# Binding the modulation's VectorE operations behind named operations, and spreading them over the block pairs

## The chip, the cores and the metric

The kernel runs on one core of a Trainium2 chip. Its time is device microseconds of one execution; several executions are shown by their median. A profiled execution leaves a trace of every instruction of the engines: TensorE (PE: matmuls; PEld: its weight loads), VectorE (DVE), ScalarE (ACT), GpSimd (POOL) and SyncE (SP, which here only issues transfers).

## The reference: what is computed

A transformer of two layers (width 1024, FFN width 2816) works on 256 latent tokens and 256 context tokens. Layer 0 mixes the tokens with a short convolution, layer 1 with grouped-query attention; an FFN stands before and after each mixer. Every sublayer is modulated by vectors that come from the conditioning:

```python
mod = (jax.nn.silu(c) @ mod_w[i] + mod_b[i]).reshape(bsz, 3, 3, 1, D_MODEL)
modc = (jax.nn.silu(c_ctx) @ mod_w[i] + mod_b[i]).reshape(3, 3, D_MODEL)
lat = lat + 0.5 * mod[:, 0, 2] * _swiglu(
    _modulate(lat, norm_g[i, 0], mod[:, 0, 0], mod[:, 0, 1]), ffn_w13[i, 0], ffn_w2[i, 0])
```

`_modulate` is an RMS norm scaled by (1 + scale) and shifted; `_swiglu(h, w13, w2)` is (silu(gate) * up) @ w2. The products are in float32. `mod` and `modc` together need nine chunks of 1024 numbers for each layer, one set for the latent and one for the context stream.

## The kernel before

**Products.** Each float32 operand is split into a high and a low part. `split` (L107) writes the high part with ScalarE (L108) and the low part with VectorE (L109), and a product is three matmuls: high by high (L137), high by low (L138), low by high (L139), in `mm3`. Weights come in as raw float32 tiles `wr` of 128x1024 (`load_raw`, L102, issued on SP at L104) from a ring of eight buffers, and are split into `wh` and `wl`.

**The FFN** (`ffn`, L768) takes the hidden blocks in three thirds of 8, 7 and 7. For each block the first product gives gate and up, VectorE multiplies them to `gm`, and `gm` is split into `gh` and `gl`. After each third, the second product (`project`, L575, accumulating in `py`) adds that third's share to all 8 output tiles m; `finish` (L553) then updates the residual `x` on VectorE (L559), gated by the modulation.

In the three FFNs with 512 tokens most blocks are computed as a "block pair" (`Pair`, L686 on): a fast-multiplication scheme with seven products of 12 matmuls of 128x256 in place of eight. Its steps `head`, `five`, `six`, `seven` and `four` are interleaved with those of the pair before. The sums of weights run on VectorE (L717, L725), a negation on POOL (L695) with a transfer issued on POOL (L698), sums of products on VectorE (L754, L759), the product `gm` (L765), then the split into `gh` and `gl`.

**The modulation.** The vectors of chunk 2 of layer 0 and later are computed by VectorE while TensorE does the FFNs. One unit, `mod_unit` (L173), is one VectorE operation of 128x1024 (L179, written out as `junk`): it multiplies a transposed weight tile with the broadcast conditioning and sums along the row into one column of `mod`. There are 224 units; two raw tiles (`load_mod`, from the same ring `wr`, issued on SP) feed four units, or two units where only the latent stream is needed.

**What sets the order.** Units wait in a list. `tick(n)` (L216) adds n to an account and issues a unit for every whole one; it is called after each block pair, after each finished tile of the second product, and in the other stages. `gate_of` and `scale_of` issue units themselves if a vector that is needed is not done. The program is written in the order of the code, but a planner then lays out each engine's instructions, by its own estimate of when operands come and engines are free; so an independent unit can land far from the place of its tick. `tc.issue_after(op)` ties instructions on the same engine to come after `op` in that engine's order, without a semaphore.

In the trace of before, the first FFN's pairs run at 96 to 115, 162 to 229 and 270 to 339 us, with second products between and after them; the convolution mixer follows to 556; the second FFN's pairs lie within 586 to 868, the third's within 937 to 1218; then come attention and the last FFN, which has half the tokens.

Of the kernel before, what the change touches and what calls it, by code (L numbers as in the profile page):

```python
# [20 lines left out]
T2 = 2 * S  # L21
# [26 lines left out]
def hybrid_kernel(ctx: ExitStack, tc: tile.TileContext, a: dict, out: bass.AP):  # L48
    nc = tc.nc
# [12 lines left out]
    def nm(s):  # L62
        uid[0] += 1
        return f"{s}{uid[0]}"
# [42 lines left out]
    def split(hi, lo, src):  # L107
        nc.scalar.activation(out=hi, in_=src, func=AF.Copy)  # L108
        return nc.vector.tensor_tensor(out=lo, in0=src, in1=hi.bitcast(F32), op=ALU.subtract)  # L109
# [63 lines left out]
    def mod_unit(l, ch, pair, raw, j, v):  # L173

        mt = mod_tile(l, ch)
        kt = pair * 2 + j
        col = ch * KT + kt
        junk = mp.tile([P, D], BF16, name=nm("junk"), tag="junk", bufs=1)
        nc.vector.tensor_tensor_reduce(  # L179
            out=junk,  # L180
            in0=raw[j],
            in1=scbc[:, v, :],
            scale=0.5 if ch in (2, 8) else 1.0,
            scalar=modb[:, l, col : col + 1],
            op0=ALU.mult,
            op1=ALU.add,
            accum_out=mt[:, kt, v : v + 1],
        )
        done[l, ch] += 1

    def streams(l, ch):
        return 1 if l == 1 and ch >= 5 else 2
# [10 lines left out]
    units = []  # L203
    owed = [0.0]

    def next_unit():
        if not units:
            l, ch, pair = jobs.pop(0)
            mod_tile(l, ch)
            raw = load_mod(l, ch, pair)  # L210
            units.extend(
                (l, ch, pair, raw, j, v) for j in range(2) for v in range(streams(l, ch))
            )
        mod_unit(*units.pop(0))

    def tick(n):  # L216

        owed[0] += n
        while (jobs or units) and owed[0] >= 1:
            owed[0] -= 1  # L220
            next_unit()
# [17 lines left out]
    def gate_of(l, j):  # L239

        ch = 3 * j + 2

        def get(m):
            while done.get((l, ch), 0) < (m // 2 + 1) * 2 * streams(l, ch):
                next_unit()
            return modv[l, ch]

        return get
# [304 lines left out]
    def finish(m, ps, c0, c1, gate, tail, wide=False):  # L553
        g = gate(m)
        for s in range(2):
            for o in [s * S - c0] if not wide else range(0, T2 if s == 0 else 0, S):
                if not c0 <= s * S < c1:
                    continue
                nc.vector.scalar_tensor_tensor(  # L559
                    out=x[:, m, s * S : s * S + S],  # L560
                    in0=ps[:, o : o + S],
                    scalar=g[:, m, s : s + 1],
                    in1=x[:, m, s * S : s * S + S],
                    op0=ALU.mult,
                    op1=ALU.add,
                )
        if tail:
            tail(m, c0, c1)

# [5 lines left out]
    def project(ws, src, nk, gate, tail, tot, late, ev, between=()):  # L575

        def products(ps, w, ks, c0, c1, wide=True):
            ms = [src(k, c0, c1) for k in ks]
            if wide and len(ms[0]) == 3:
                return mm_wide(ps, [w(k) for k in ks], ms, ks[0] == 0, ks[-1] == nk - 1)
            for k, m in zip(ks, ms):
                mm3(ps[:, : c1 - c0], w(k), m[:2], k == 0, k == nk - 1)

        nf = 3 if between else 2
        ahead = {}  # L590

        def get(m):
            for i in range(m, min(m + 3, KT)):
                if i not in ahead:
                    ahead[i] = ws(i)
            return ahead[m]

        w2 = [get(m) for m in range(nf)]
        p2 = [psum("py") for _ in range(nf)]
        cut = nk - 2 if between else nk - 1  # L600
        for i in range(nf):
            products(p2[i], w2[i], range(cut), 0, tot)
            if i < len(between):
                between[i]()
        if between:
            for i in range(nf):
                products(p2[i], w2[i], (nk - 2,), 0, tot)
        for i in range(nf):
            products(p2[i], w2[i], (nk - 1,), 0, tot)
            finish(i, p2[i], 0, tot, gate, tail, len(src(0, 0, tot)) == 3)  # L610
            tick(ev)

        for m in range(nf, KT - late):
            if tail and tot == S and m == KT - 2:
                ready()
            w = get(m)
            ps = psum("py")
            wide = len(src(0, 0, tot)) == 3 and m < KT - 1
            products(ps, w, range(nk), 0, tot, wide)
            finish(m, ps, 0, tot, gate, tail, wide)  # L620
            if m < (5 if late else 6):
                tick(ev)
        if late:

            wl = [get(m) for m in (6, 7)]
            if tail:
                ready()
            for s in range(2):
                for i in range(2):
                    ps = psum("py")  # L630
                    products(ps, wl[i], range(nk // 2), s * S, s * S + S)
                    flush(1)
                    products(ps, wl[i], range(nk // 2, nk), s * S, s * S + S)
                    finish(6 + i, ps, s * S, s * S + S, gate, tail)
# [12 lines left out]
    def w13_post(pp, g, c0, c1):  # L647
        n = c1 - c0
        sg = tp.tile([P, T2], F32, name=nm("sg"), tag="sg", bufs=3)
        nc.scalar.activation(out=sg[:, :n], in_=pp[0][:, :n], func=AF.Silu)  # L650
        gm = tp.tile([P, T2], F32, name=nm("gm"), tag="gm", bufs=3)
        nc.vector.tensor_tensor(out=gm[:, :n], in0=sg[:, :n], in1=pp[1][:, :n], op=ALU.mult)
        split(g[0][:, c0:c1], g[1][:, c0:c1], gm[:, :n])

    def beside_post(pp, g):

# [25 lines left out]
    class Pair:  # L682
# [80 lines left out]
        def four(self, g):  # L763
            self.prod(self.p, "A22", "T4", False)
            nc.vector.tensor_tensor(out=self.gm, in0=self.sg, in1=self.u, op=ALU.mult)  # L765
            split(g[0], g[1], self.gm)

    def ffn(l, b, h, tot, gate, tail, gs=(), ev=(0, 0), z=None):  # L768
        gs = list(gs)
        i0 = 0  # L770
        for t, n in enumerate(THIRDS):
            between = ()
            if tot == T2:
# [22 lines left out]
                for i in range(len(gs), n):  # L796
                    if t == 0 and not heads and i in AS_IS[l, b]:
                        w = load_w(a["w13"][l, b, i])
                        pp = psum("pg"), psum("pu")
                        if prev:  # L800
                            prev.seven()
                        if "T1" not in h.t:
                            with tc.issue_after(rows["W1"]):
                                h.sums()
                        w13_mm(pp, w, h, range(4), 0, T2)
                        if prev:
                            gs.append(new_pair("g"))
                            prev.four(gs[-1])
                            prev = None
                        w13_mm(pp, w, h, range(4, KT), 0, T2)  # L810
                        gs.append(new_pair("g"))
                        w13_post(pp, gs[-1], 0, T2)
                        tick(3)
                        continue
                    if heads:
                        pr = heads.pop(0)
                    else:
                        pr = Pair(a["w13"][l, b, i0 + i], h)
                        pr.sums(0)
                        pr.sums(1)  # L820
                        pr.head()
                    pr.five()
                    if prev:
                        prev.seven()
                    pr.six()
                    if prev:
                        gs.append(new_pair("g"))
                        prev.four(gs[-1])
                    prev = pr
                    tick(0.5)  # L830

                def last():
                    gs.append(new_pair("g"))
# [46 lines left out]
    h = Plain()  # L880
# [121 lines left out]
    ws, gs0, raws, cut = {}, [], {}, {}  # L1002
# [47 lines left out]
    h = FirstBlocks(h, h32)  # L1050
# [13 lines left out]


    hn = Plain()
    ffn(0, 0, h, T2, gate_of(0, 0), tail_norm(0, 1, hn), gs0, (2.9, 2.4))
    h = hn

    zs = []  # L1070
    for m in range(KT):
# [30 lines left out]
        z = tp.tile([P, T2], F32, name=nm("z"), tag="sg", bufs=3)  # L1102
        nc.vector.tensor_tensor(out=z, in0=d, in1=pb, op=ALU.mult)
        zs.append(new_pair("z"))
        split(zs[m][0], zs[m][1], z)
        tick(5)

    def by_pairs(key, box=None):
# [10 lines left out]
    hn = Blocks()  # L1119
# [3 lines left out]
    )  # L1123
    h = hn
    hn = Blocks()
    ffn(0, 1, h, T2, gate_of(0, 2), tail_norm(1, 0, hn), (), (2.7, 2))
    h = hn


    hn = Plain()  # L1130
    ffn(1, 0, h, T2, gate_of(1, 0), tail_norm(1, 1, hn), (), (2.5, 1.6))
    h = hn
    ap = ctx.enter_context(tc.tile_pool(name="ap", bufs=2))

# [240 lines left out]
    hn, hz = Beside(), Early()  # L1375
# [88 lines left out]
```

## Time and profile before

| | before |
|---|---|
| median of 3 runs | 1572.37 us (1571.88 to 1573.98) |
| the profiled execution | 1566.88 us, span 1565.1 us |
| PE busy | 1550.9 us, 99% |
| VectorE busy | 1284.6 us, 82% |
| ScalarE busy | 778.7 us, 50% |
| GpSimd busy | 223.5 us, 14% |

All the profile's times are within the span, from the first to the last instruction. A row of a group gives source line, engine, operation, output and inputs, shape, count, then total and mean busy time and the idle time in front of it with what ended it. A row of waits gives the engine and line, what it waited for, the microseconds in total, the number of waits and the longest. A timeline row gives start and duration, and in brackets how long the engine had been idle and what released it.

### The profile page before, as it was taken

What the parts mean: (1) busy time and instruction counts of PE and PEld (TensorE: products, weight loads), DVE (VectorE), ACT (ScalarE), POOL (GpSimd) and SP (SyncE); (2) the same over time, 40 slices, a digit from 0 to 9 for tenths busy, and PEclk for the clock granted to TensorE, in tenths of its full rate; (3) what the DMA queues carried; (4) which work ended last, traced back from release to release, by engine and by line L of the source; (5) the groups of instructions that cost most, each with busy time, mean ns of one, the idle gap of its engine ahead of it and who ended that gap; (6) DMA issues with size and microseconds to landing.
All of it is one profiled execution on the core that took longest, in us unless ns stands there. A gap on an engine that the chain in (4) does not pass through costs nothing.

```text
span 1565.1 us, 26349 instructions
## 1 busy us (share of the span) xinstructions
PE 1550.9 (99%) x10282; PEld 1420.6 (91%) x10282; DVE 1284.6 (82%) x2023; ACT 778.7 (50%) x1289; POOL 223.5 (14%) x188
## 2 busy tenths in 40 slices
PE   9999999999999999999999999999999999999999
PEld 7888998999888899989999899989899889898888
DVE  5978889789997678987987988977978887887676
ACT  5632552644423366436345476436446355774553
POOL 0103203200000121141131112131131003300000
PEclk9999999999999999999999999999999999999999
DMA  9657457564564434664664734665775753356562
GB/s 376 217 167 205 122 165 201 115 191 163 188 205 173 128 75 122 196 174 110 200 169 122 213 71 124 204 165 123 246 179 153 248 177 102 100 189 211 174 196 74
DMA packets 88253, 263.53 MB, mean 168 GB/s; under 512 B 10816, under 2 KB 12608, under 8 KB 88128
## 3 DMA queue, kind: packets, MB, share of 16 engines
q1 hardware_dynamic: 69408, 230.72, 44.5%
q0 software_dynamic: 16128, 29.37, 11.1%
q10 hardware_dynamic: 2592, 1.76, 0.4%
q8 instruction: 80, 1.31, 0.3%
q14 instruction: 45, 0.37, 0.1%
HBM read 259.45 MB, written 1.05 MB: 166 GB/s over the span
## 4 chain that ended last, share of the span: by engine, by line
PE 86%; DVE 8%; issue 2%; ACT 2%; DMA 2%; POOL 0%; POOLq 0%; DVEq 0%; ACTq 0%; SPq 0%
PE py L137 7%; PE py L138 7%; PE py L139 7%; PE p L137 6%; PE p L139 6%; PE p L138 6%; PE q L137 5%; PE q L139 5%; PE q L138 5%; PE py L145 2%; PE pg L145 2%; PE pu L145 2%; DVE junk L179 2%; DVE wl L109 2%; DMA wr<-in_modT 1%
## 5 line engine op out<-in xcount | busy, mean ns | idle before, releaser
L108 ACT ACTIVATE wh<-wr 128x1024 fp32r<-128x1024 f32 (+2 forms) x446 | 394.7, 913 | 320.7 <-PE py L138 129.4
L109 DVE TENSOR_TENSOR wl<-wr,wh 128x1024 fp32r<-128x1024 f32 (+2 forms) x446 | 456.8, 1048 | 111.9 <-ACT wh L108 92.0
L179 DVE CUSTOM_DVE_ANT_0 junk<-wr,scbc,modb 128x1024 bf16<-128x1024 f32 x222 | 285.8, 1287 | 33.5 <-DMA wr<-in_modT 30.9
L137 PE MATMUL py<-gh,wh 128*128 128x512 f32 (+1 forms) x570 | 213.5, 375 | 0.0
L138 PE MATMUL py<-gl,wh 128*128 128x512 f32 (+1 forms) x570 | 213.2, 374 | 0.0
L139 PE MATMUL py<-gh,wl 128*128 128x512 f32 (+1 forms) x570 | 213.0, 374 | 0.0
L695 POOL TENSOR_SCALAR wr<-wr 128x512 f32<-128x512 f32 x56 | 99.3, 1774 | 718.7 <-DMA wr<-in_w 256.0
L559 DVE SCALAR_TENSOR_TENSOR x<-py,mod,x 128x256 f32<-128x256 f32 x213 | 94.0, 476 | 41.3 <-PE py L139 29.9
L137 PE MATMUL p<-th,wh 128*128 128x256 f32 x448 | 126.8, 283 | 0.0
L138 PE MATMUL p<-tl,wh 128*128 128x256 f32 x448 | 126.8, 283 | 0.0
L139 PE MATMUL p<-th,wl 128*128 128x256 f32 x448 | 126.8, 283 | 0.0
L139 PEld LDWEIGHTS py<-gh,wl 128*128 128x128 f32 x570 | 107.3, 188 | 19.1
L137 PEld LDWEIGHTS py<-gh,wh 128*128 128x128 f32 x570 | 107.4, 188 | 18.4
L138 PEld LDWEIGHTS py<-gl,wh 128*128 128x128 f32 x570 | 107.4, 188 | 18.0
L115 POOL DMA_DIRECT2D w4l<-in_w x56 | 53.1, 948 | 271.8 <-ACT w4l L114 197.6
L137 PE MATMUL q<-bh,wh 128*128 128x256 f32 x320 | 90.9, 284 | 0.6 <-ACT wh L108 0.4
L139 PE MATMUL q<-bh,wl 128*128 128x256 f32 x320 | 90.8, 284 | 0.0
L138 PE MATMUL q<-bl,wh 128*128 128x256 f32 x320 | 90.5, 283 | 0.0
L138 PEld LDWEIGHTS p<-tl,wh 128*128 128x128 f32 x448 | 86.0, 192 | 0.3
L137 PEld LDWEIGHTS p<-th,wh 128*128 128x128 f32 x448 | 86.0, 192 | 0.3
L139 PEld LDWEIGHTS p<-th,wl 128*128 128x128 f32 x448 | 86.0, 192 | 0.0
L108 ACT ACTIVATE gh<-gm 128x512 fp32r<-128x512 f32 x66 | 41.2, 624 | 71.3 <-DVE gm L765 67.9
(304 smaller groups left out, 4054.8 us busy)
## 6 DMA issues: line engine op xcount, KB each, us to landing
wr<-in_modT SPq DMA_DIRECT2D x126, 512.0 KB, 4.8
wr<-in_w SPq DMA_DIRECT2D x120, 512.0 KB, 4.4
wr<-in_w2b SPq DMA_DIRECT2D x64, 448.0 KB, 4.0
wr<-in_w2a SPq DMA_DIRECT2D x32, 512.0 KB, 5.1
wr<-in_w SPq DMA_DIRECT2D x56, 256.0 KB, 4.1
wr<-in_w POOLq DMA_DIRECT2D x56, 256.0 KB, 5.0
w4l<-in_w POOLq DMA_DIRECT2D x56, 256.0 KB, 6.0
pm<-in_mod SPq DMA_DIRECT2D x16, 512.0 KB, 10.2
```

The costliest lines, as they stand in the source:

```text
L108: nc.scalar.activation(out=hi, in_=src, func=AF.Copy)
L109: return nc.vector.tensor_tensor(out=lo, in0=src, in1=hi.bitcast(F32), op=ALU.subtract)
L115: nc.gpsimd.dma_start(out=lo, in_=src, accum_op=ALU.add)
L137: nc.tensor.matmul(ps, wh, mh, start=first, stop=False, **kw)
L138: nc.tensor.matmul(ps, wh, ml, start=False, stop=False, **kw)
L139: nc.tensor.matmul(ps, wl, mh, start=False, stop=last, **kw)
L145: nc.tensor.matmul(ps, w[0], m[2], start=first and n == 0, stop=False)
L179: nc.vector.tensor_tensor_reduce(out=junk, in0=raw[j], in1=scbc[:, v, :], scale=0.5 if ch in (2, 8) else 1.0, scalar=modb[:, l, col : col ...
L559: nc.vector.scalar_tensor_tensor(out=x[:, m, s * S : s * S + S], in0=ps[:, o : o + S], scalar=g[:, m, s : s + 1], in1=x[:, m, s * S : s * ...
L695: nc.gpsimd.tensor_scalar(out=r1[:, :T2], in0=r2[:, :T2], scalar1=-1.0, scalar2=None, op0=ALU.mult)
```

## The change

Four operations are recorded in a list `place` as they are issued: the last x update of a tile in `finish`, the VectorE half of the split of a hidden block in `w13_post` and in `Pair.four`, and of the split of a block `z` of the convolution mixer. `next_unit` wraps each modulation unit in `tc.issue_after(place[-1])`, so that its operation comes on VectorE's queue behind the latest of them. The transfers of the unit's weights are issued on SP and are not tied by this.

The amounts of `tick` are changed with it: a block pair owes 1.5 units in place of 0.5; a finished tile of the second product owes 1.8 in the first two thirds and 1.3 in the last (2.9 and 2.4 before) in the first FFN, 1.6 and 1 (2.7 and 2; 2.5 and 1.6) in the other two. Where a project ends with its last two tiles done in halves (`late` is 2), tiles up to m = 3 tick in place of those up to m = 4. The total of units is the same.

```diff
+    place = []
+
     def next_unit():
...
-        mod_unit(*units.pop(0))
+        if place:
+            with tc.issue_after(place[-1]):
+                mod_unit(*units.pop(0))
+        else:
+            mod_unit(*units.pop(0))
...
-                nc.vector.scalar_tensor_tensor(
+                ins = nc.vector.scalar_tensor_tensor(
                     out=x[:, m, s * S : s * S + S],
...
+                place.append(ins.ins)
...
-            if m < (5 if late else 6):
+            if m < 6 - late:
                 tick(ev)
...
-        split(g[0][:, c0:c1], g[1][:, c0:c1], gm[:, :n])
+        place.append(split(g[0][:, c0:c1], g[1][:, c0:c1], gm[:, :n]).ins)
...
-            split(g[0], g[1], self.gm)
+            place.append(split(g[0], g[1], self.gm).ins)
...
-                    tick(0.5)
+                    tick(1.5)
...
-    ffn(0, 0, h, T2, gate_of(0, 0), tail_norm(0, 1, hn), gs0, (2.9, 2.4))
+    ffn(0, 0, h, T2, gate_of(0, 0), tail_norm(0, 1, hn), gs0, (1.8, 1.3))
...
-        split(zs[m][0], zs[m][1], z)
+        place.append(split(zs[m][0], zs[m][1], z).ins)
...
-    ffn(0, 1, h, T2, gate_of(0, 2), tail_norm(1, 0, hn), (), (2.7, 2))
+    ffn(0, 1, h, T2, gate_of(0, 2), tail_norm(1, 0, hn), (), (1.6, 1))
...
-    ffn(1, 0, h, T2, gate_of(1, 0), tail_norm(1, 1, hn), (), (2.5, 1.6))
+    ffn(1, 0, h, T2, gate_of(1, 0), tail_norm(1, 1, hn), (), (1.6, 1))
```

## The prediction

> **What bounds the kernel now.** I read the page first: the busy times, the chain that ended last, and the groups of the operations that the change moves.
>
> ```profile
> span 1565.1 us, 26349 instructions
> ...
> PE 1550.9 (99%) x10282; PEld 1420.6 (91%) x10282; DVE 1284.6 (82%) x2023; ACT 778.7 (50%) x1289; POOL 223.5 (14%) x188
> ...
> L179 DVE CUSTOM_DVE_ANT_0 junk<-wr,scbc,modb 128x1024 bf16<-128x1024 f32 x222 | 285.8, 1287 | 33.5 <-DMA wr<-in_modT 30.9
> ...
> wr<-in_modT SPq DMA_DIRECT2D x126, 512.0 KB, 4.8
> wr<-in_w SPq DMA_DIRECT2D x120, 512.0 KB, 4.4
> wr<-in_w2b SPq DMA_DIRECT2D x64, 448.0 KB, 4.0
> ```
>
> TensorE (PE) is busy 99% of the span, so only its 14.2 idle microseconds (1565.1 less 1550.9), and the few that a restart hides in a busy record, can be won; but VectorE (DVE) with 82% can easily become the second bound. The modulation (L179, "junk") is 222 recorded operations of 1.287 us. Next came the waits, for what stops TensorE and what stops VectorE ahead of a modulation.
>
> ```profile
> PE q L137 <- ACT gm L748: 2.7, 3, 2.1
> PE ss L274 <- DVE acc L265: 1.5, 1, 1.5
> ...
> DVE junk L179 <- DMA wr<-in_modT: 30.9, 28, 5.3
> ```
>
> VectorE stands 28 times, 30.9 us in all, in front of a modulation whose weights have not landed. TensorE's steady-state idle time is much smaller, and its two largest pieces are in the first two lines. The timelines of both places show the cause; the first, in us:
>
> ```profile
> 97.68 1.28 DVE L179 CUSTOM_DVE_ANT_0 junk<-wr,scbc,modb 128x1024 bf16<-128x1024 f32 x1 [5.28 <-DMA wr<-in_modT]
> ...
> 101.30 0.68 DVE L717 TENSOR_TENSOR wr<-wr 128x512 f32<-128x512 f32 x1
> ...
> 102.15 1.06 ACT L108 ACTIVATE wh<-wr 128x1024 fp32r<-128x1024 f32 x1 [1.91 <-DVE wr L717]
> 103.12 0.35 ACT L748 COPY gm<-q 128x256 f32<-128x256 f32 x1
> ...
> 101.19 0.28 PE L139 MATMUL p<-th,wl 128*128 128x256 f32 x1
> 103.52 0.39 PE L137 MATMUL q<-hh,wh 128*128 128x256 f32 x1 [2.06 <-ACT gm L748]
> ```
>
> VectorE waits 5.28 us for modulation weights; so its sum L717 is late, ScalarE's (ACT) copy behind it waits, and TensorE starts 2.33 us after its last issue where 0.12 is its pace (84 matmuls of a pair in 10.08 us). That is a loss of 2.2. The second and third places:
>
> ```profile
> 1254.99 0.28 PE L139 MATMUL py<-gh,wl 128*128 128x256 f32 x1
> 1255.12 1.28 DVE L179 CUSTOM_DVE_ANT_0 junk<-wr,scbc,modb 128x1024 bf16<-128x1024 f32 x1 [2.33 <-DMA wr<-in_modT]
> 1256.81 0.38 PE L274 MATMUL ss<-ones,acc 128*128 128x1 f32 x2 [1.54 <-DVE acc L265]
> ...
> 805.35 0.28 PE L139 MATMUL p<-th,wl 128*128 128x256 f32 x1
> 805.88 0.39 PE L137 MATMUL q<-bh,wh 128*128 128x256 f32 x1 [0.25 <-ACT gm L748]
> ```
>
> At 1255 the loss is 1.82 − 0.12 = 1.7 us, again behind a modulation that waits for its transfer; at 805 it is 0.53 − 0.12 = 0.4, first pair of a third, behind a bunch of modulations.
>
> **The change part by part.**
>
> Nothing is added or removed: the orders of both kernels hold the same 224 modulations, the same matmuls and the same transfers. TensorE's order differs only in about 200 places near the joins of stages, and I cost that at zero: the same operands are ready there.
>
> *The binding.* A modulation now comes on VectorE's queue after a named operation: the last x update of a tile (L559), the split of a finished block product. Before, the planner put it where its own clock saw room, with its load close ahead. Counting in the two orders, the SP queue issues a modulation's load a median of 31.8 us before VectorE comes to it, against 8.7 before; the smallest leads are 8.2 and 4.4, and the landing row says 4.8. So the 30.9 us of waits should all but vanish. What that gives on TensorE is only what was late next. At 101: four modulations (4 × 1.2 at their issue spacing) stand among the sums of the second pair, but adding the spacings of after's queue the next needed split ends 0.6 us ahead of its matmul, so nothing replaces the wait: −2.2. At 1255: after's order has no modulation near the end of that stage: −1.7. At 805: 1.06 us of room at the split that counts: −0.4. Bounds of the sum: 0 (something else is late there) and −4.3; I take −4.3, because the queue sums leave room at each.
>
> *Three times as many per pair* (0.5 to 1.5 owed). In before the pairs of a steady stretch held none. A windows row of such a stretch (its length, then busy time of PE, of weight loads, of DVE, ACT and POOL), and the part of one pair into which the new modulation goes, right after the split gl (L109):
>
> ```profile
> 280.00:320.00 40.00, 40.00 (x336) 40.00 (x335) 29.11 (x38) 24.54 (x44) 7.52 (x7) 1.00 0.48 122
> ```
> ```profile
> 290.25 0.68 DVE L109 TENSOR_TENSOR gl<-gm,gh 128x512 fp32r<-128x512 f32 x1
> 291.46 2.43 DVE L109 TENSOR_TENSOR wl<-wr,wh 128x1024 fp32r<-128x1024 f32 x3 [0.52 <-ACT wh L108]
> 293.81 0.68 DVE L717 TENSOR_TENSOR wr<-wr 128x512 f32<-128x512 f32 x1
> ```
>
> That is 29.11 / 40 × 10.08 = 7.3 us of VectorE per pair (336 matmuls, four pairs). With 1.5 × 1.29 = 1.9 it is 9.2 of 10.08, 92%: a pair with two modulations takes 9.9, the next with one 8.6. Behind the modulation on VectorE's queue stand the weights' low halves for products that TensorE reaches 1.5 us or more later (sums over after's queue in the steady pairs). So in the steady stretch I take 0; if that cover were gone, each of the 56 pairs would pay up to one modulation, 1.29.
>
> *First pairs of a third.* There the queue carries the backlog of the project before it and the splits of two pairs. In before:
>
> ```profile
> 592.05 2.43 DVE L109 TENSOR_TENSOR wl<-wr,wh 128x1024 fp32r<-128x1024 f32 x3 [0.34 <-ACT wh L108]
> ...
> 595.61 1.21 DVE L725 TENSOR_TENSOR wr<-wr,wr 128x1024 f32<-128x1024 f32 x1
> 596.74 3.69 DVE L109 TENSOR_TENSOR wl<-wr,wh 128x1024 fp32r<-128x1024 f32 x4
> ```
>
> VectorE runs here from 592.05 to 600.4 without a gap, and after's order puts two modulations in. Adding the spacings, a split is 0.4 us late for its matmul at 599; the same sum gives 0.4 at 366, in the last second product of the first FFN, and 0.04 to 0.3 of room at 274, 281 and 943. I take +0.8, with bounds 0 and 8 such places × 1.29 = 10.3.
>
> *Fewer per tile of the second product* (2.9 and 2.4 to 1.8 and 1.3, and so on; the condition on m drops one tile's tick at four ends). VectorE in a second product has room: TensorE needs a tile's result only three tiles later. Gain 0 beyond what is counted; a loss would be at 366 above.
>
> *The queues of SP and POOL.* Earlier loads hold the ring of eight raw buffers longer. In after's order the shortest time from a free buffer to ScalarE's reading is 4.3 us, at weights of the second product, against 4.0 to land (the w2b row). TensorE reads 8 us or more after ScalarE. So 0, bounds 0 and a microsecond at each of a few places; that lies inside the 10.3.
>
> *POOL beside a fuller VectorE.* Each pair has one multiplication on POOL (L695).
>
> ```profile
> 282.84 1.65 POOL L695 TENSOR_SCALAR wr<-wr 128x512 f32<-128x512 f32 x1 [5.06 <-DMA wr<-in_w]
> 283.05 1.10 DVE L717 TENSOR_TENSOR wr<-wr 128x512 f32<-128x512 f32 x1
> ...
> 294.92 1.48 POOL L695 TENSOR_SCALAR wr<-wr 128x512 f32<-128x512 f32 x1 [3.96 <-DVE p L759]
> ```
>
> Where both meet, VectorE's L717 took 1.10 where its row at 293.81 has 0.68, and POOL's operation 1.65 for 1.48: VectorE lost 0.42 us. That fits into the 0.9 us that an average pair has left, so 0 here.
> [...]
>
> **Sum**: −2.2 − 1.7 − 0.4 + 0.8 = −3.5 us. The profiled execution took 1566.88 us (its span plus 1.8), 5.5 under the median of the runs, 1572.37. So 1563.4 for such an execution, 1568.9 for the median.
>
> **The rivals.**
>
> *The stalls only move* (no change, 1572). The first pairs of the eight thirds lose about half a microsecond each, 8 × 0.5 = 4, as much as the two transfer waits gave back. For it: the rooms of 0.04 to 0.3 us above. Against it: later pairs recover, and a late split costs only its excess.
>
> *VectorE becomes the bound in the pairs* (slower). If a POOL multiplication met in each pair costs VectorE its whole 1.48 us, then 7.3 + 1.9 + 1.48 = 10.7 against 10.08, 0.6 lost per pair with such a meeting. It decides from 0.9 us of loss per pair upwards; about half of the 56 multiplications fall in pairs, 28 × 0.6 = 17, so 1589. Against it: 0.42 was lost in the meeting shown. [...]
>
> *One modulation too many at each start of a third* (slower): 10.3 us, less the 4.3 won, gives 1578. For it: modulations now stand between the sums that the first pairs need at once.
>
> *The change does nothing:* excluded by the order, where VectorE's queue differs throughout.
>
> **How the numbers follow.** Forecast 0.48, stalls move 0.25, POOL against VectorE 0.14, starts of thirds 0.13. Two per thousand, 3.1 us, is about what a measurement can tell: faster 0.48, same 0.25, slower 0.27. The forecast's own range is 1564 to 1569.2: with the 0.8 not paid it is 1568.1, and about 10 of TensorE's 14.2 idle microseconds are not in my sum, of which I let 4 more go. The range for 8 in 10 goes up to 1582, past the thirds' rival and toward the other.
>
> **What would show it.** Right: no line for modulations waiting on their transfer, VectorE about 92% busy in 280 to 320 with TensorE at 40.00, no gap at 101 and 1255. Wrong: TensorE waiting for q, p or weights' halves inside pairs, POOL's group of L695 well above the 1.48 to 1.65 shown, or waits of TensorE at the first pairs that add up to more than 4 us.

## The result and the profile after

The changed kernel took 1576.16 us (median of 20 runs, 1570.93 to 1580.86), the kernel before 1571.74 us beside it (20 runs, 1565.94 to 1576.12): a ratio of 1.0028, with a 95% interval of 1.0016 to 1.0040. It is slower by some 4.4 us, where 3.5 us of gain were forecast.

Its profiled execution took 1573.85 us. The two profiled executions lie further apart than the medians: that of before ran 4.9 us below its median, with TensorE's clock granted in full (1.000 in the mean), that of the changed kernel 2.3 below, at 0.999. The page, with the rows that answer to those of before:

```profile
span 1571.8 us, 26308 instructions
...
PE 1555.0 (99%) x10282; PEld 1421.8 (90%) x10282; DVE 1287.0 (82%) x2023; ACT 776.3 (49%) x1289; POOL 224.5 (14%) x188
...
L179 DVE CUSTOM_DVE_ANT_0 junk<-wr,scbc,modb 128x1024 bf16<-128x1024 f32 x222 | 289.2, 1303 | 1.5
```

The last number of the L179 row is VectorE's idle time in front of the modulation: 33.5 us before, 1.5 now. The binding does what it says. The waits show what came in its place (engine and line, what it waited for, us in all, times, longest):

```profile
ACT wh L108 <- DMA wr<-in_w: 18.2, 6, 7.0
ACT wh L108 <- DMA wr<-in_w2b: 17.9, 4, 7.4
...
DVE wr L724 <- DMA wr<-in_w: 6.7, 6, 2.9
...
PE q L139 <- DVE wl L109: 3.4, 5, 1.5
```

In the kernel before the first, second and fourth of these waits do not occur, and the third is 0.3 us in all: ScalarE (wh) and VectorE (L724, the sum at L717 before) now stand in front of block weights that have not landed, and TensorE in front of their low halves.

Both executions issue the same 10282 matmuls. The difference between the two start times of the matmul of the same number, followed along the span, gives where the time went; each line is what that difference gained or lost within the stretch (times of before, us):

```
  90- 110  wait for modulation weights, first FFN      -2.1
 265- 284  first pairs of a third, first FFN           +0.7
 370- 384  end of the first FFN, the convolution's norm +0.9
 584- 602  first pairs, second FFN                     +1.7
 800- 810  first pair of a third, second FFN           -0.5
 900- 920  norm between second and third FFN           +1.8
1150-1163  first pairs of a third, third FFN           +4.1
1195-1218  later pairs of that third                   +0.9
1250-1275  end of the third FFN, norm                  -1.9
   0-  13  first transfers                             +0.5
1300-1400  attention, start of the last FFN            +0.7
  rest of the span                                     -0.1
  sum                                                  +6.7
```

The last three rows are listed apart because they belong to no step. Everything else happens in these few places; in between the two kernels run alike. The lines for 0 to 13 and 1300 to 1400 differ among runs of other variants by as much. The predicted gains are there: 2.1 us at 101, 0.5 at 805 and 1.9 behind 1250. The losses are larger, and the two largest places begin with late weights. The first, at 1152 to 1169 (rows of SP, VectorE and TensorE, start and duration, in brackets the idle time before and its releaser; then a windows row, whose last numbers are TensorE's granted clock, the DMA share and GB/s):

```profile
1130.85 3.92 SPq L104 DMA_DIRECT2D wr<-in_modT  x2
...
1137.05 0.33 SPq L104 DMA_DIRECT2D wr<-in_w  x1
1138.25 0.33 SPq L700 DMA_DIRECT2D wr<-in_w  x1
1140.24 1.33 SPq L104 DMA_DIRECT2D wr<-in_modT  x2
1143.23 0.33 SPq L104 DMA_DIRECT2D wr<-in_w  x1
1144.64 0.33 SPq L700 DMA_DIRECT2D wr<-in_w  x1
...
1144.95 0.91 POOL L705 DMA_DIRECT2D wr<-in_w  x1 [0.41 <-POOL wr L702]
...
1152.65 0.69 DVE L724 TENSOR_TENSOR wr<-wr 128x512 f32<-128x512 f32 x1 [2.85 <-DMA wr<-in_w]
...
1157.64 1.28 DVE L179 CUSTOM_DVE_ANT_0 junk<-wr,scbc,modb 128x1024 bf16<-128x1024 f32 x1
...
1159.45 1.28 DVE L179 CUSTOM_DVE_ANT_0 junk<-wr,scbc,modb 128x1024 bf16<-128x1024 f32 x1
...
1161.26 1.10 DVE L724 TENSOR_TENSOR wr<-wr 128x512 f32<-128x512 f32 x1
...
1165.48 0.54 PE L139 MATMUL q<-th,wl 128*128 128x256 f32 x1 [1.46 <-DVE wl L109]
```
```profile
1164.00:1169.00 5.00, 3.54 (x17) 3.52 (x17) 4.46 (x6) 3.04 (x6) 0.01 (x1) 0.66 0.80 173
```

In the kernel before, the weights of the same two pairs (counted along each queue) and their sums stand here:

```profile
1125.81 0.33 SPq L693 DMA_DIRECT2D wr<-in_w  x1
...
1129.17 0.33 SPq L693 DMA_DIRECT2D wr<-in_w  x1
```
```profile
1138.80 1.09 DVE L717 TENSOR_TENSOR wr<-wr 128x512 f32<-128x512 f32 x1
...
1152.59 0.68 DVE L717 TENSOR_TENSOR wr<-wr 128x512 f32<-128x512 f32 x1
```

The weights of both pairs (1137.05 and 1138.25, then 1143.23 and 1144.64) are issued 12 to 15 us later than before, behind modulation transfers, and the ring is fuller: counted from both traces, a modulation tile keeps its buffer for a median of 11 us before and 35 now, from its issue to its last unit, and within 1100 to 1160 the modulation holds 2.1 of the eight buffers on average before and 4.6 now. POOL's transfer for the first pair (L705, 1144.95) then takes 7.6 us to land, where the median of the 56 is 5.0. VectorE idles 2.85 us in front of the first pair's sum, then finds two modulations in its queue; so the second pair's sum comes at 1161.26, and the low half that TensorE needs comes after 1.5 us of idle time. Then TensorE's clock is granted at 0.66 over five microseconds: matmuls that follow each other every 0.12 us come every 0.21 us for 3.3 us, which costs another 1.4.

The second, at the norm before the third FFN:

```profile
897.87 2.97 SPq L104 DMA_DIRECT2D wr<-in_modT  x2
903.34 0.33 SPq L104 DMA_DIRECT2D wr<-in_w  x1
```
```profile
909.79 0.63 ACT L113 ACTIVATE w4h<-wr 128x512 fp32r<-128x512 f32 x1 [1.89 <-DMA wr<-in_w]
910.46 0.63 ACT L114 ACTIVATE w4l<-w4h 128x512 fp32r<-128x512 f32 x1
911.00 0.49 ACT L396 ACTIVATE bh<-t,mod 128x256 fp32r<-128x256 f32 x1
```
```profile
913.28 0.38 PE L137 MATMUL pg<-bh,wh 128*128 128x256 f32 x1 [0.36 <-ACT bh L396]
...
914.14 0.39 PE L138 MATMUL pg<-bl,wh 128*128 128x256 f32 x1 [0.48 <-DVE bl L397]
```

Here ScalarE's queue holds the norm's first output (bh) behind the split of a block weight that is late by 1.89 us and that TensorE needs only a pair later. In the kernel before no modulation transfer stands on SP in that stretch and the norm's bh comes first.

The third kind is VectorE's own backlog, without any late transfer:

```profile
591.50 1.63 DVE L179 CUSTOM_DVE_ANT_0 junk<-wr,scbc,modb 128x1024 bf16<-128x1024 f32 x1
...
594.20 1.27 DVE L179 CUSTOM_DVE_ANT_0 junk<-wr,scbc,modb 128x1024 bf16<-128x1024 f32 x1
```
```profile
594.33 0.39 PE L139 MATMUL q<-bh,wl 128*128 128x256 f32 x1 [0.57 <-DVE wl L109]
...
600.41 0.39 PE L139 MATMUL q<-th,wl 128*128 128x256 f32 x1 [0.53 <-DVE wl L109]
```

The steady pairs lost nothing but the tail of such a place (280.43, 0.30 us of idle time); VectorE is busy 36.03 of 40 us:

```profile
280.00:320.00 40.00, 39.70 (x331) 39.57 (x330) 36.03 (x51) 23.45 (x41) 12.08 (x11) 1.00 0.66 166
```

### The profile page after: what moved, and what is told of

Same layout as the page of the kernel before. It is cut to its first block, busy times and chain, and to the rows that moved or that the text cites. A ratio compares the mean times of both kernels' runs of the same rounds, so it can differ in the third digit from the quotient of the medians.

```text
span 1571.8 us, 26308 instructions
## 1 busy us (share of the span) xinstructions
PE 1555.0 (99%) x10282; PEld 1421.8 (90%) x10282; DVE 1287.0 (82%) x2023; ACT 776.3 (49%) x1289; POOL 224.5 (14%) x188
## 4 chain that ended last, share of the span: by engine, by line
PE 87%; DVE 6%; DMA 3%; ACT 2%; issue 1%; POOL 0%; POOLq 0%; ACTq 0%; DVEq 0%; SPq 0%
PE py L137 8%; PE py L138 8%; PE py L139 8%; PE p L137 6%; PE p L139 6%; PE p L138 6%; PE q L139 5%; PE q L137 4%; PE q L138 4%; DMA wr<-in_w 2%; PE py L145 2%; PE pu L145 2%; PE pg L145 2%; DVE wl L109 1%; PE pv L138 1%; PE pv L137 1%
## 5 line engine op out<-in xcount | busy, mean ns | idle before, releaser
L109 DVE TENSOR_TENSOR wl<-wr,wh 128x1024 fp32r<-128x1024 f32 (+2 forms) x446 | 462.6, 1057 | 69.9 <-ACT wh L108 48.8
L179 DVE CUSTOM_DVE_ANT_0 junk<-wr,scbc,modb 128x1024 bf16<-128x1024 f32 x222 | 289.2, 1303 | 1.5
L702 POOL TENSOR_SCALAR wr<-wr 128x512 f32<-128x512 f32 x56 | 101.4, 1810 | 780.6 <-DMA wr<-in_w 577.5
L732 DVE TENSOR_TENSOR wr<-wr,wr 128x1024 f32<-128x1024 f32 x56 | 69.4, 1238 | 1.0
```

The source lines that it names most:

```text
L179: nc.vector.tensor_tensor_reduce(out=junk, in0=raw[j], in1=scbc[:, v, :], scale=0.5 if ch in (2, 8) else 1.0, scalar=modb[:, l, col : col ...
L702: nc.gpsimd.tensor_scalar(out=r1[:, :T2], in0=r2[:, :T2], scalar1=-1.0, scalar2=None, op0=ALU.mult)
L732: tt(out=v(r2), in0=v(r2), in1=s2.unsqueeze(1).to_broadcast([P, 2, T2]), op=ALU.subtract,)
```

## The experiments

Theory L: bound units hold buffers of the shared ring from their early fetch to their late use, so block weights land late. Theory V: units in VectorE's queue ahead of the first pairs' splits make these late. Every variant is planned anew, so places that an edit doesn't touch move too, by some microseconds in all; a verdict rests on the place, read as in the list above, where the total doesn't carry it. Each place is read from one execution, and a loss can hold slow matmuls at the halved clock, as at 1165 (granted at 0.50); where it does, the text says how much, counted from the spacing of the matmuls (1.4 to 1.6 us for each 3.4 us of halved clock in most cases). Ratios are against the kernel before, run beside each; the diffs are against the changed kernel, and shortened.

**The binding alone.** The amounts as before:

```diff
-                    tick(1.5)
+                    tick(0.5)
-gs0, (1.8, 1.3))    and (1.6, 1), (1.6, 1), m < 6 - late
+gs0, (2.9, 2.4))    and (2.7, 2), (2.5, 1.6), m < (5 if late else 6)
```

> The binding alone: units tied behind the named operations as in the changed kernel, but owed as in the kernel before (0.5 per block pair, 2.9 to 1.6 per tile of the second product). Theory L (late weights): the binding lets a unit's weights be fetched about 31 us before VectorE uses them, they hold buffers of the shared ring, and block weights land late. This order has the same long leads (median 30.7 us), so it loses as much as the changed kernel or more: 1575 to 1580 us, with ScalarE or VectorE waiting on weight transfers. Theory V (VectorE backlog by the extra units in the pairs): few units stand among pairs, so the loss goes: 1569 to 1573 us, no gaps near 594 and 600.

It took 1631.7 us, 1.038 (1.036 to 1.040): 61 us lost, far beyond both theories. The largest gap:

```profile
277.12 1.27 DVE L179 CUSTOM_DVE_ANT_0 junk<-wr,scbc,modb 128x1024 bf16<-128x1024 f32 x1
...
278.32 0.47 DVE L565 SCALAR_TENSOR_TENSOR x<-py,mod,x 128x256 f32<-128x256 f32 x1
278.72 1.27 DVE L179 CUSTOM_DVE_ANT_0 junk<-wr,scbc,modb 128x1024 bf16<-128x1024 f32 x1
...
281.52 1.28 DVE L109 TENSOR_TENSOR wl<-wr,wh 128x512 fp32r<-128x512 f32 x2
```
```profile
282.25 0.58 PE L139 MATMUL p<-hh,wl 128*128 128x256 f32 x1 [7.29 <-DVE wl L109]
```

Between 262 and 281.5 us VectorE runs x update, modulation, x update, modulation, and the split of the next third's first weight stands behind all of them. That is theory V at its purest, at the join of second product and pairs; in the same trace ScalarE waits 107 us for weights (57.9, 27.9 and 21.3 in three groups), which is theory L.

**The amounts alone.**

```diff
-        if place:
+        if False:
             with tc.issue_after(place[-1]):
```

> The new amounts alone (1.5 per pair, fewer per tile), no binding. Theory L: the planner puts loads close ahead of the units again (median lead 6.5 us in this order, against 31.7 with the binding), the ring is free for block weights, so about 1570 to 1573 us, like the kernel before or a little better, with VectorE waiting again some 30 us on modulation transfers. Theory V: as many units are owed in the pairs as in the changed kernel, so 1574 to 1578 us with gaps at the first pairs of thirds.

1588.24 us, 1.010 (1.008 to 1.012). Theory L's number was missed, though the ring was about as free as it said (ScalarE waits only 2.8 us for wh weights): free units in the pairs wait for their own transfers, and VectorE's queue with them.

```profile
DVE junk L179 <- DMA wr<-in_modT: 64.4, 46, 5.4
```

So neither half of the change is good without the other: the binding needs fewer units per tile, and more units per pair need the binding (or earlier loads, which was not tested).

**No unit after a third's first pair.**

```diff
-                    tick(1.5)
+                    if prev:
+                        tick(1.75)
```

> The changed kernel, but no unit is owed after the first pair of a third (later pairs owe 1.75). Theory V: the gaps at the first pairs (272 to 281, 594 to 600) close, 2 to 3 us less than the changed kernel: 1572 to 1574 us. Theory L: loads and ring are as before this edit (median lead 31.3 us, weights short as often), so 1575 to 1577 us; where a weight tile is late the gap stays.

1581.09 us, 1.006 (1.004 to 1.009): worse than both expected. The gaps at 594 and 600 are gone, as theory V said (584 to 602 loses 0.0 in place of 1.7, and 265 to 284 gains 0.6), but at 1150 to 1163 late weights now cost 7.0 us (2.5 of them slow matmuls), and 5.1 us went at the end of the convolution (2.8 slow matmuls):

```profile
1156.97 0.69 DVE L724 TENSOR_TENSOR wr<-wr 128x512 f32<-128x512 f32 x1 [4.35 <-DMA wr<-in_w]
```
```profile
1158.86 0.39 PE L137 MATMUL q<-th,wh 128*128 128x256 f32 x1 [1.50 <-ACT wh L108]
...
1161.94 0.58 PE L139 MATMUL q<-th,wl 128*128 128x256 f32 x1 [2.58 <-DVE wl L109]
```

**A ring of its own for the modulation** (two buffers, the shared ring six):

```diff
-            return [load_raw(src[:, j * D : j * D + D]) for j in range(2)]
+            raw = [mp.tile([P, D], F32, name=nm("mr"), tag="mr", bufs=2) for _ in range(2)]
+            for j in range(2):
+                nc.sync.dma_start(raw[j], src[:, j * D : j * D + D])
+            return raw
-        ... tag="wr", bufs=8)
+        ... tag="wr", bufs=6)
```

> The changed kernel, but the modulation's weights get a ring of two buffers of their own and the shared ring has six in place of eight. Theory L: the modulation can no longer hold more than two buffers (median lead 13.9 us), so the gaps at 911 to 921 and 1158 to 1168 go: 1569 to 1573 us, unless six buffers are too few for the weights. Theory V: VectorE's work and its places are the same, so 1574 to 1577 us.

1575.21 us, 1.0025 (1.0014 to 1.0035), no better. ScalarE's wh waits for weights are all but gone (0.5 us), but with only two buffers the modulation's transfers are late again (20.7 us of VectorE's time in 19 waits), and 1150 to 1163 still loses 4.6, 900 to 920 3.3 (1.5 of them slow matmuls). The lateness has only moved from one kind of weight to the other, so this run decides nothing.

**Half of the modulation's transfers**, in the binding alone and in the changed kernel (one weight tile is used twice and the other left out, so these two are probes and no kernels to use):

```diff
-            return [load_raw(src[:, j * D : j * D + D]) for j in range(2)]
+            return [load_raw(src[:, :D])] * 2
```

> The binding alone, as in the first of these runs (1631.7 us), but each modulation job fetches one weight tile and uses it for both of its halves: half the transfers and half the buffers held, the same VectorE operations in the same places (half of the modulation's sums come out wrong, it is a probe). Theory L (bound units hold ring buffers, block weights land late): most of the 61 us go: 1585 to 1600 us. If VectorE's order alone were the cause (theory V): 1625 to 1635 us.

1618.24 us, 1.030 (1.028 to 1.032): 13 us of the 61 go, not most of them, while the gap at 282 keeps 7.0 us of its 7.3. In the binding alone VectorE's order is the larger part, and both theories' numbers were wrong.

> The changed kernel with one weight tile per job in place of two, as above. Theory L: ScalarE's waits for weight transfers go and with them the gaps at 911 to 921 and 1158 to 1168: 1567 to 1572 us, the kernel before or better. Theory V: VectorE's work and places are the same, so 1574 to 1577 us, with the gaps at 272, 594 and 600 still there.

1569.22 us, 0.9985 (0.9975 to 0.9994): 7 us better than the changed kernel, as theory L had it, and faster than the kernel before, which the forecast wanted. ScalarE no longer waits for the weights of a wh at all, and 1150 to 1163 loses 0.3 in place of 4.1 us, 1195 to 1218 nothing; 584 to 602 still loses 1.7, theory V's part. At 900 to 920, against what I expected, 2.9 us are lost (1.6 of them slow matmuls), with ScalarE's w4h (L113) still waiting for its weight.

**Short modulation operations, all transfers** (a probe too: the sums leave out seven eighths of the columns).

```diff
-            out=junk,
-            in0=raw[j],
-            in1=scbc[:, v, :],
+            out=junk[:, :128],
+            in0=raw[j][:, :128],
+            in1=scbc[:, v, :128],
```

> The changed kernel with all its transfers, but each modulation operation reads 128 of 1024 columns (the sums leave out the rest, a probe): some 0.2 us of VectorE in place of 1.2. Theory V: all gaps at first pairs go: 1566 to 1571 us. Theory L: the weights are as late as before, gaps at 911 to 921 and 1158 to 1168 stay: 1573 to 1577 us.

1578.17 us, 1.0047 (1.0032 to 1.0062). With the modulation's time on VectorE cut from 289 to 85 us (0.38 us an operation, more than the 0.2 I had expected) the kernel is not faster at all. The gaps at 272 to 281, 594 and 600 are gone, so theory V is right for these places; the late weights remain and grow:

```profile
DVE wr L724 <- DMA wr<-in_w: 32.6, 11, 7.3
```

900 to 920, 1150 to 1163 and 1195 to 1218 lose 4.2, 3.7 and 4.6 us (1.4 to 1.6 of each slow matmuls); all else is as good as before or better.

**Bound four named operations back.**

```diff
-            with tc.issue_after(place[-1]):
+            with tc.issue_after(place[-4]):
```

> The changed kernel, but a unit is tied behind the fourth last of the named operations in place of the last, so it runs up to three block pairs earlier and frees its buffers earlier (median lead of its load 19.4 us in this order, against 31.7). Theory L: weights get their leads back, 1568 to 1573 us. Theory V: the units still stand among the pairs' operations, 1574 to 1578 us.

1575.45 us, 1.0027 (1.0016 to 1.0038). ScalarE's wh waits for the weights of the FFN (in_w, in_w2a and in_w2b) fall from 47.9 to 15.5 us, and 1150 to 1163 loses only 0.7; but a late weight in front of the norm makes 900 to 920 lose 7.8 us (2.9 of them slow matmuls):

```profile
908.00 0.63 ACT L113 ACTIVATE w4h<-wr 128x512 fp32r<-128x512 f32 x1 [5.41 <-DMA wr<-in_w]
```

The median lead of a transfer, by which I had expected 1568 to 1573, doesn't tell the worst one.

**One tile at a time.** A unit's weight tile is fetched with its own first unit:

```diff
+        if j not in raw:
+            raw[j] = load_raw(a["modT"][l, ch * 4 + pair][:, j * D : j * D + D])
```

> The changed kernel, with the same transfers, but a unit's weight tile is fetched when its own first unit comes and not both tiles of a job together: a buffer is held for two units in place of four, with all the traffic left. If theory L's cost is that of held buffers: 1570 to 1573 us. If it is that of the transfers' place on SP's queue and their traffic, which stay (median lead 29.6 us in this order): 1574 to 1577 us.

1574.58 us, 1.0019 (1.0008 to 1.0029), inside the second case. By place both cases have a part: 900 to 920 lost 0.4 in place of 1.8 and 1195 to 1218 0.2. But 1150 to 1163 kept 2.5, which is what the changed kernel loses there without its slow matmuls, so the stall itself stayed; and 3.8 us were lost anew at the end of the convolution, 1.5 of them slow matmuls. The rows of that place show a late weight again, in front of the norm's squares (L267):

```profile
550.64 0.63 ACT L113 ACTIVATE w4h<-wr 128x512 fp32r<-128x512 f32 x1 [5.61 <-DMA wr<-in_w]
...
552.65 0.61 ACT L267 ACTIVATE sq<-x 128x512 f32<-128x512 f32 x1
...
555.50 0.38 PE L284 MATMUL ss<-ones,acc 128*128 128x1 f32 x2 [1.44 <-DVE acc L275]
```

**Only the units of pairs and convolution bound.**

```diff
-                place.append(ins.ins)
+                place.clear()
```

> The changed kernel, but units owed in a second product are free again; only those owed in pairs and in the convolution are tied. Theory L: the leads stay long (median 29.5 us), weights of the second product are short less often (1 of 96 under 6 us against 8), so a little better than the changed kernel, 1571 to 1575 us. Theory V: units at the end of a second product can again drop into VectorE's idle time ahead of the first pair, so the gaps at 272 and 594 shrink: 1571 to 1574 us.

1573.84 us, 1.0015 (1.0004 to 1.0026), the best of the complete variants and still not the kernel before. 265 to 284 now gains 0.6 and 370 to 384 loses 0.2 in place of 0.9, so these two losses came from units tied behind the last x updates; 1150 to 1163 loses nothing: the weights of its two pairs are issued from 1126.27 to 1134.52, some 10 us earlier than in the changed kernel. Left are 1.7 at 584 to 602, 3.8 at 900 to 920 and 4.5 at 1195 to 1218 (1.5 and 1.4 of the last two slow matmuls), where a sum waits for its weights again:

```profile
1212.96 0.69 DVE L724 TENSOR_TENSOR wr<-wr 128x512 f32<-128x512 f32 x1 [3.49 <-DMA wr<-in_w]
```

Both expectations held in total, so the total doesn't separate them.

**One unit per pair.**

```diff
-                    tick(1.5)
+                    tick(1.0)
-gs0, (1.8, 1.3))    and (1.6, 1), (1.6, 1)
+gs0, (2.35, 1.85))  and (2.15, 1.5), (2.05, 1.3)
```

> The changed kernel with 1.0 unit per pair and per tile half way between old and new (2.35 and 1.85; 2.15 and 1.5; 2.05 and 1.3). Binding with the old amounts took 1631.7 us, with the new ones 1576.2. If units stacked behind the last tiles' x updates and ahead of the next third's first weights (theory V) make that difference: between, 1590 to 1610 us, with the gap at the joins of second product and pairs. If it is late weights alone (theory L; the leads are 31.3 us here as there): 1575 to 1585 us.

1589.74 us, 1.011 (1.010 to 1.013): between 1631.7 and 1576.2, and the gap at the join of second product and pairs is there with 2.5 us at 273, where the binding alone has 7.6 and the changed kernel none. So the lowered amounts per tile are what makes the binding bearable.

**No unit in the second FFN's last second product.**

```diff
-    ffn(0, 1, h, T2, gate_of(0, 2), tail_norm(1, 0, hn), (), (1.6, 1))
+    ffn(0, 1, h, T2, gate_of(0, 2), tail_norm(1, 0, hn), (), (1.85, 0))
```

> The changed kernel, but the second FFN's last second product owes no unit (its other tiles 1.85 in place of 1.6), so that no modulation transfer stands on SP ahead of the next FFN's first weights (in this order these weights are issued some 8 us earlier). Theory L for the gaps at 911 to 921: ScalarE's wait for the weight tile at 909.8 goes and the gaps with it, 1.5 to 2.5 us less: 1573.5 to 1575 us, and no loss in that place in the trace. If the norm itself is late for another reason the place still loses 1.8.

1575.62 us, 1.0019 (1.0008 to 1.0031). The total is hardly better, since 1195 to 1218 loses 2.8 us in place of 0.9 and the start of the kernel 2.0 (1.3 of them slow matmuls); but the place in question is settled. SP's rows show the weights ahead, the modulation's transfers behind:

```profile
895.21 0.33 SPq L700 DMA_DIRECT2D wr<-in_w  x1
896.88 0.33 SPq L104 DMA_DIRECT2D wr<-in_w  x1
900.17 0.33 SPq L700 DMA_DIRECT2D wr<-in_w  x1
904.87 9.63 SPq L104 DMA_DIRECT2D wr<-in_modT  x2
```
```profile
911.42 0.51 ACT L396 ACTIVATE bh<-t,mod 128x256 fp32r<-128x256 f32 x1 [1.51 <-DVE t L307]
```

The split that was 1.89 us late runs at 901.29, the norm's bh waits for its own operand only, and 900 to 920 loses nothing (−0.1 in place of +1.8).

**The places taken out one by one**, with the binding kept in pairs and convolution: no unit in the second FFN's last second product; one tile at a time; both.

```diff
-                place.append(ins.ins)
+                place.clear()
-    ffn(0, 1, h, T2, gate_of(0, 2), tail_norm(1, 0, hn), (), (1.6, 1))
+    ffn(0, 1, h, T2, gate_of(0, 2), tail_norm(1, 0, hn), (), (1.85, 0))
+        if j not in raw:
+            raw[j] = load_raw(a["modT"][l, ch * 4 + pair][:, j * D : j * D + D])
```

> Only the units of pairs and convolution bound (1573.8 us), and no unit owed in the second FFN's last second product. Theory L: the 3.8 us lost at 907 to 919 with the first of these edits go, since the weights there are issued ahead of the modulation's transfers again; what the third FFN's last third loses (4.5 us) may stay: 1569.5 to 1572 us. If the norm's lateness there comes from VectorE: unchanged, 1573 to 1575 us.

> Only the units of pairs and convolution bound, and one weight tile fetched at a time. Theory L: with single tiles both late-weight places shrink, as with single tiles alone (0.4 us at 907 to 919, 0.2 at 1206 to 1215): 1567 to 1571 us, the gap at 594 to 600 (1.7 us) left. If held buffers and bunched transfers do not matter: 1573 to 1575 us.

> All three edits: units of pairs and convolution bound, single tiles, none owed in the second FFN's last second product. Theory L: no late weight left at the three places, so the gains at 101, 276, 805 and 1256 stand against 1.7 us at 594 to 600 and little else: 1566 to 1570 us, below the kernel before. If planning anew opens other places: 1571 to 1575 us.

They took 1570.71 us, 0.9995 (0.9984 to 1.0006); 1574.02, 1.0010 (0.9994 to 1.0026); and 1570.29, 1.0000 (0.9986 to 1.0013). By place, in us against the kernel before:

```
                     265-284  584-602  900-920  1150-1163  1195-1218  1250-1275
changed kernel         +0.7     +1.7     +1.8      +4.1       +0.9       -1.9
pairs bound only       -0.6     +1.7     +3.8       0.0       +4.5       +0.3
 and none in the last  -0.6     +1.7     -0.1       0.0       +2.4       +0.6
 and one tile          -0.6     +1.7     +1.2       0.0        0.0       +0.3
 and both              -0.6     +1.7     -0.1       0.0       +0.5       +1.4
```

Each place goes as theory L has it: modulation transfers out of the way of the norm's weights, no loss at 900 to 920; single tiles, none or little at 1195 to 1218. The totals of the second and third run miss their expectations, because new losses opened elsewhere: 4.7 and 2.8 us at the end of the convolution (2.9 and 1.4 of them slow matmuls), and in the third run 1.6 of slow matmuls within 1250 to 1275. Two of the three are 5.5 to 6 us better than the changed kernel, and none is faster than the kernel before beyond its interval; with free units in the last second product the gain at 1255 goes too.

## Why the prediction was wrong

**The binding's gains: right.** VectorE's waits on modulation transfers fell from 30.9 us to almost nothing, and the three places gave 2.1, 1.9 and 0.5 us, 4.5 where 4.3 were forecast.

**The steady pairs: right.** VectorE is 90% busy there (92% forecast), and no pair of the steady stretch pays. The rival by which VectorE becomes the bound in all pairs did not come: the POOL multiplications (L702 after, L695 before) took 1.81 us in the mean against 1.77. (As a sign of being wrong, "well above the 1.48 to 1.65 shown" was badly chosen: these operations took 1.48 to 2.53 us in the kernel before already.)

**First pairs of a third: mechanism right, size wrong.** The term was +0.8. The stretches 265 to 284, 370 to 384 and 584 to 602 lost 3.3 us; with the units shortened they gain 0.35 in all. The rooms that I counted there were hundredths to tenths of a microsecond, and one modulation beside POOL's multiplication took 1.63 us for 1.28: the kind of meeting that I had priced at nothing.

**"The queues of SP and POOL ... So 0": this step failed.** I compared the shortest lead (4.3 us) with the landing time (4.0), and trusted that TensorE reads 8 us after ScalarE. Four things broke it. Modulations that VectorE reaches late free their buffers late (35 us for 11), and SP issued the weights for the sums at 1152 and 1161 12 to 15 us later than in the kernel before. POOL's transfer at 1144.95, issued among others, landed later than the median (7.6 us for 5.0), and the sum at 1152.65 needs more than one landing: its data came through two transfers and a multiplication on POOL. What stands behind a late weight is not only that weight's own product: ScalarE's queue held the norm, VectorE's queue the sums of the next pair. And the backlog so made met bound modulations, which no longer give way. Together 900 to 920 and 1150 to 1163 lost 5.9 us. Halving the modulation's transfers took 3.8 of the 4.1 at 1150 to 1163 away; moving them behind the weights took away all of the 1.8 at 900 to 920, in three kernels.

**The clock: not in the sum.** 1.4 of the 4.1 us are slow matmuls after the stall, a cost that none of my terms had. The granted clock differs from one execution to the next (0.995 to 1.000 in the mean over 29 of the kernel before), as the last section shows, so this part belongs to the profiled execution and not surely to the median.

Of the rivals "the stalls only move" came nearest in kind: the gains were given back, but more by late weights than by the first pairs alone. The measured 1576.2 lies inside the range of 1564 to 1582, on the side to which I gave 0.27, but that is no merit of the sum: the range was that wide for rivals on VectorE, and the term that decided stood in it as 0.

The new losses at the end of the convolution in four variants are of the same kind as at 900 to 920, as far as the rows tell: in each of them ScalarE's queue holds a weight split (L113) that is 4.0 to 5.6 us late ahead of the norm's squares; no run took this cause away by itself. What stays open: the 0.9 us at 1195 to 1218 in the changed kernel itself were not taken apart. A variant that keeps the gains without the losses was not found; only the probe with half of the transfers was faster than the kernel before.

## What to carry to other kernels

An ordering edge that delays the use of a prefetched tile also lengthens the life of its buffer (here from a median of 11 us to 35) and leaves its transfer where it was: count whom the transfer now precedes, not only whether the waiting engine has its data. When leads are compared with landing times, take the worst tile and everything queued behind it on the engine that first touches it. A binding and the amounts it orders have to be judged together: each half alone cost 17 to 61 us here, and both together 4.

## What the runs showed of the hardware

A short stall of TensorE cost twice in the changed kernel: 1.6 us of extra time at 1165 were followed by 16 matmuls at 0.21 us in place of 0.12, with a granted clock of 0.50 from 1165.6 to 1169.0. In the binding alone the matmuls behind the stall of 7.29 us at 282.25 come every 0.21 us too, up to 286.90; such matmuls cost that run some 18 us in all, counted from their spacing, and its granted clock was 0.984 in the mean. But not every stall was followed by them: the kernel before lost 2.2 us at 103 and 1.7 at 1257 with no slow matmul behind, and the same stall of 1.62 us at that place in the runs with one tile at a time and with none in the last third had none either. What decides it no run shows.

One kernel's executions differ with the clock they get: of 29 executions of the kernel before, run beside the last three variants, those with a mean granted clock of 1.000 took 1566.3 to 1568.3 us and those with 0.996 took 1571.6 to 1575.2. The profiled execution of before had no halved stretch until its last matmul, which ends at 1561.7 us; the clock of 0.50 stands there from 1563.6 on.

A VectorE operation beside one on POOL took longer in the changed kernel, but not by the whole of the other: the modulation at 591.5 took 1.63 us in place of 1.28, while POOL's multiplication from 590.6 on took 2.33, where the shortest in the kernel before took 1.48.
